# Program order and a new product order at the seams of a Transformer block on one Trainium2 core

## Chip, cores and metric

One core of one Trainium2 chip runs the kernel in one launch. The metric is the device time in microseconds (us); lower is better. TensorE (PE) does the matmuls, VectorE (DVE), ScalarE (ACT) and GpSimd (POOL) prepare operands and finish results, and SyncE (SP) issues most DMAs.

## The reference

One encoder block on x of 1024 tokens x 1024, float32. What matters here is its second half:

```python
merged = sigmoid(ga) * (att @ w_att_up) + sigmoid(gh) * (rec @ w_hgrn_up)
h = layer_norm(ALPHA * h + merged @ w_o, ln1_g, ln1_b)
gate, up = split(h @ w_ffn_in, 2)                      # 1024 x 2816 each
h = layer_norm(ALPHA * h + (silu(gate) * up) @ w_ffn_out, ln2_g, ln2_b)
```

## The kernel before

**Products.** Every float32 operand is split into a high part (a cast to fp32r, on ACT) and a low part (operand less high part, on POOL or DVE: `split`, L201). `mm3` (L227) multiplies high x high, high x low and low x high. The feed-forward projections don't multiply blocks as they are: they use Strassen's scheme in Winograd's form, with seven products in the place of eight, numbered 1 to 7 (`PRODUCTS`, L1258), of sums and differences of blocks. For the input projection the sums of h are b11, b21, t1, t2, b22, t3, t4 (`xb`), those of the weights a11, a12, s1 to s4, a22.

**Output projection** (`phase2`). `wo_chunk` (L1134) loads and splits w_o in chunks of 128 columns. For each tile t of 128 rows two `half`s of 24 matmuls run, then `rest(t, y)` does the first layer norm, transposes the row tile on TensorE in eight 128x128 blocks, evacuates them (`tsv`; `on_act` says which on ACT), and `h1_blocks` makes of them the blocks of the next projection: t1 and t2 at once, b22, t3 and t4 through a store and a load (`td`, `t_raw`). At tile 7 products 1 and 2 of the first two feed-forward groups are started ahead of `rest`.

**Feed-forward input** (`ffn_in`). There are 22 groups, each of two weight columns of 128 (`f_raw`) and seven products of 12 matmuls. `wino_project` (L1319) gives a group in parts; the next group's product 5 stands ahead of the last product, 4, of the one before. `keep` copies a bank to `wkeep`; `evac` makes silu(gate) x up, and `combine` (L1416) the sums a11, a12, a22, s1 to s4 for the last projection, which go to DRAM (`gd`).

**Last projection** (`out_begin`, `ffn_out`). The six products in `OUT_ORDER` have 11 steps each (j = 0 to 10, 66 in all; a step is four `mm3`, 12 matmuls). `sums(s + 2)` and `prep(s + 2)` prepare the weights two steps ahead: a DVE sum, `w_hi` on ACT, `w_lo` on POOL; `acts` loads the activations, for products 5, 7 and 3 split already, as `ghi` and `glo` on the queue of SP. Product 3, the last one, makes beside it the blocks t4 for product 4 (`later`: `t4hi` on ACT, `t4lo` on DVE). Then product 4 runs a row tile at a time for rows 4 to 7. `add` takes the banks to the rows `y2`, `stat` their statistics; `finish` (L1617) is the layer norm of a row tile: a power on POOL, an activation on ACT, a multiply by g2 on POOL (L1629), an add of b2 on DVE (L1630), a store. Row 7 is done on DVE alone. Rows 0 to 6 finish beside product 4.

**What sets the order.** Up to the last projection a scheduler places instructions by its own rules and the given priorities (`high_priority`). From `ffn_out` on `in_order` (L1483) keeps each engine, SP's queue too, to the order in which the code records.

Of the kernel before, what the change touches and what calls it, by code (L numbers as in the profile page):

```python
# [10 lines left out]
F32 = mybir.dt.float32  # L11
# [70 lines left out]
class Block:  # L82
# [1051 lines left out]
    def wo_chunk(self, hl, c):  # L1134
# [5 lines left out]
        self.split(hi[:, :, s], lo[:, :, s], raw)  # L1140

    def phase2(self):
        nc = self.nc
        gc, bc = self.col["g1"], self.col["b1"]
        with ExitStack() as es:
# [54 lines left out]
            raws = []  # L1200

            def rest(t, y):

                with self.tc.high_priority(offset=2 * self.evac_ahead if t == 7 else 0):
                    mv = self.stats(yp, y, "1")
                    if t == 7:
                        nc.vector.tensor_scalar(y, y, mv[:, 0:1], mv[:, 2:3], op0=OP.subtract, op1=OP.mult)
                    else:
                        self.normalise(yp, y, y, mv)
                    on = (0, 1, 3, 4, 6, 7) if 4 <= t < 7 else (1, 3, 4, 6)  # L1210
                    self.h1_blocks(yp, t, lambda q, v=None: self.transposed(yp, y, q, gc, bc, v, on_act=on),
                                   last=t >= 3)
                nc.scalar.dma_start(self.n1_d[t], y)

            for t in range(8):
                ms = []
                for k0 in (0, 4):
# [8 lines left out]
                    ms += [(mh[:, k, :], ml[:, k, :]) for k in range(4)]  # L1226
                y = yp.tile([128, D], F32, name="y1", tag="y1", bufs=2)
                nc.sync.dma_start(y, self.ahs_d[t])

                def half(hh, y=y, ms=ms, t=t):  # L1230
                    ps = self.ps_pj()
                    for k, (mh, ml) in enumerate(ms):
                        whi, wlo = (z[:, k, :] for z in wo[hh])
                        self.mm3(ps, mh, ml, whi, wlo, k == 0, k == KT - 1)
                    s = slice(HALF * hh, HALF * (hh + 1))
                    with self.tc.high_priority(offset=self.evac_ahead if t == 7 else 0):
                        nc.vector.scalar_tensor_tensor(y[:, s], ps, 0.5, y[:, s], op0=OP.mult, op1=OP.add)

                half(0)
                if t == 0:  # L1240
                    second = half, y
                    continue
                if t == 1:
                    second[0](1)
                    rest(0, second[1])
                half(1)
                if t in (5, 6):
                    raws.append(self.ffn_raws(FS[t - 5]))
                if t == 7:
                    self.first_groups = [self.wino_project(raws[f], lambda *a, f=f: self.first_evac[f](*a), 1 + f)  # L1250
                                         for f in range(2)]
                    for g in self.first_groups:
                        next(g)
                rest(t, y)


# [7 lines left out]
    def h1_blocks(self, pool, t, v, last=False):  # L1264
# [9 lines left out]
        if t < 4:  # L1274
            for i, n in enumerate(("b11", "b21")):
                put(n, v(i))
            return
# [14 lines left out]
        less(t1, b12, 0, "b11")  # L1292
        b22 = v(1)
        nc.vector.tensor_sub(t2, b22, t1)
        put("t2", t2)
        put("t1", t1)
        t3 = tmp()
        (nc.vector if last else nc.gpsimd).tensor_sub(t3, b22, b12)
        later(1, "t3", t3)
        later(0, "b22", b22)  # L1300

        t4 = tmp()
        hi, lo = (z[:, :, c].bitcast(F32) for z in self.xb["b21"])
        nc.vector.tensor_sub(t4, hi, t2)
        nc.vector.tensor_add(t4, t4, lo)
        later(2, "t4", t4)
# [12 lines left out]
    def wino_project(self, raws, evac, ahead=0):  # L1319

# [6 lines left out]
        banks = {}  # L1327

        def product(n, bank, first):
            a, b = self.PRODUCTS[n]  # L1330
            hi, lo = self.granules()
            self.split(hi, lo, self.wino_a(A, a))
            xhi, xlo = self.xb[b]
            if first:
                banks[bank] = self.ps_pj() if (bank == 2) != (ahead == 2) else self.ps_sd()
# [6 lines left out]
        def keep(ps):  # L1342
            with self.tc.high_priority(offset=self.evac_ahead):
                t = self.ws.tile([128, HALF], F32, name="wkeep", tag="wkeep", bufs=3)
# [7 lines left out]
        if not ahead:  # L1352
            m5 = keep(product(5, 2, True))
            yield
        m1 = keep(product(1, 1, True))
        c11 = product(2, 3, True)
        if ahead:
            yield
            m5 = keep(product(5, 2, True))
        out(0, 0, c11, m1)  # L1360
        u2 = keep(product(6, 1, False))
        out(0, 1, product(3, 2, False), u2)
# [12 lines left out]
    def ffn_in(self):  # L1375

        nc = self.nc
        with ExitStack() as es:
# [37 lines left out]
            def combine(j, second):  # L1416
# [8 lines left out]
                whole("a12", j, a12)  # L1425
                parts("a22", j, a22)
                s1, s2, s4 = (small(n) for n in ("s1", "s2", "s4"))
                nc.vector.tensor_add(s1, a21, a22)
                nc.vector.tensor_sub(s2, s1, a11)
                nc.vector.tensor_sub(s4, a12, s2)  # L1430
                whole("s2", j, s2)
                parts("s1", j, s1)
                parts("s4", j, s4)

            def vecs(v):
                t = fp.tile([128, D], F32, name=f"ab{len(ab)}")
# [4 lines left out]
            for i, n in enumerate(("b22", "t3", "t4")):  # L1441
                for k in range(4):
                    r = small("t_raw", F32 if k % 2 else F32R).bitcast(F32)
                    nc.sync.dma_start(r, self.td[i][:, k, :])
                    hi, lo = self.xb[n]
                    self.split(hi[:, k, :], lo[:, k, :], r, eng_lo="dve")
            ab = []
            held = None
            for p in range(NF):
                if p > 1:  # L1450
                    grp = self.wino_project(nxt, evac_of(FS[p]))
                    next(grp)
                else:
                    grp = self.first_groups[p]
                if 1 < p + 1 < NF:
                    nxt = self.ffn_raws(FS[p + 1])
                if held:
                    next(held, None)
                    combine((p - 1) // 2, (p - 1) % 2)
# [12 lines left out]
            self.out_begin()  # L1472
            next(held, None)
            combine(NJ - 1, 1)
# [3 lines left out]
    OUT_ORDER = (1, 2, 6, 5, 7, 3)  # L1478
# [4 lines left out]
    def in_order(self):  # L1483
# [4 lines left out]
        for i in traced[n:]:  # L1488
            before = self.lasts.get(i.engine)
# [18 lines left out]
    def out_begin(self):  # L1508

        self.W = W = {}  # L1510
        for i in range(2):
            r = self.wraw.tile([128, D], F32, name="w_raw", tag="wraw", bufs=2)
            for k in range(2):
# [246 lines left out]
```

## Time and profile before

| | us |
|---|---|
| median of 3 runs (lowest to highest) | 2146.92 (2145.78 to 2148.17) |
| the profiled execution | 2148.89 |
| its span | 2147.1 |
| TensorE busy | 2032.1 (95%) |
| VectorE, ScalarE, GpSimd busy | 1394.1, 918.8, 1214.0 |
| mean granted TensorE clock | 0.984 |

Times in the profile are counted from the span's start. A row of an engine has start, duration, engine, line, operation, output and inputs, and in brackets the idle time before it and what ended it. Matmuls are pipelined, so a matmul's duration is longer than the distance to the next.

### The profile page before, as it was taken

The page shows a single profiled execution, that of the slowest core. Times are in us where ns is not written, and L with a number is a line of the kernel's source. Part 1 is how long each engine was busy: PE and PEld are TensorE (multiplying, and loading weights), DVE is VectorE, ACT ScalarE, POOL GpSimd, SP SyncE. Part 2 cuts the span into 40 slices and gives each one's busy share as a digit, 9 for nine tenths or more (in the row PEclk, how much of TensorE's full clock was granted, in tenths as well). Part 3 has the DMA queues.
Part 4 walks back from the last instruction along what each step waited for, and adds up shares of the span by engine and source line. Part 5 has one row for each costly group of instructions (what it writes and reads, how often), then busy time and mean ns, then how long its engine had stood idle before and what let it go on. Part 6 is the DMA issues. An engine that isn't in the chain of part 4 may idle for free.

```text
span 2147.1 us, 31283 instructions
## 1 busy us (share of the span) xinstructions
PE 2032.1 (95%) x10941; PEld 1675.5 (78%) x10941; DVE 1394.1 (65%) x2165; ACT 918.8 (43%) x1870; POOL 1214.0 (57%) x960
## 2 busy tenths in 40 slices
PE   4789999989999999999999899998999999999997
PEld 3678887878778888778888688876788888878876
DVE  7666746876458854778535723347778788867655
ACT  6534455444554435544354432144434344344322
POOL 3465653666535764466644854343567677754554
PEclk9899999999999999999999999999999999999999
DMA  5333442434324453333444764344535444458584
GB/s 205 102 125 103 133 155 93 144 111 158 128 89 143 132 164 121 113 123 117 152 127 137 264 204 157 97 138 141 178 118 177 152 158 158 142 173 292 197 264 156
DMA packets 296447, 324.20 MB, mean 151 GB/s; under 512 B 15905, under 2 KB 212834, under 8 KB 296290
## 3 DMA queue, kind: packets, MB, share of 16 engines
q1 hardware_dynamic: 288832, 296.81, 43.1%
q10 hardware_dynamic: 7458, 25.40, 3.0%
q8 instruction: 86, 1.41, 0.3%
q14 instruction: 71, 0.58, 0.1%
HBM read 211.78 MB, written 110.36 MB: 150 GB/s over the span
## 4 chain that ended last, share of the span: by engine, by line
PE 59%; DVE 5%; issue 4%; DMA 4%; POOL 3%; ACT 2%; SPq 0%; DVEq 0%; ACTq 0%; POOLq 0%
PE pj L229 12%; PE pj L230 12%; PE pj L231 12%; PE sd L231 5%; PE sd L229 5%; PE sd L230 5%; POOL w_lo L208 2%; PE sd L1023 1%; ACT p L801 1%; DVE p L823 1%; DMA wa<-in_w_in_dram 1%; POOL y L1629 1%; DVE hR L984 0%; DMA binb<-in_ln_in_b_dram 0%; PE sd L628 0%
## 5 line engine op out<-in xcount | busy, mean ns | idle before, releaser
L208 POOL TENSOR_TENSOR w_lo<-wa,w_hi 128x512 fp32r<-128x512 f32 x276 | 386.7, 1409 | 278.4 <-ACT w_hi L204 249.2
L204 ACT CAST w_hi<-wa 128x512 fp32r<-128x512 f32 x276 | 170.1, 618 | 230.9 <-PE pj L230 163.6
L208 POOL TENSOR_TENSOR w_lo<-wsum,w_hi 128x512 fp32r<-128x512 f32 x88 | 135.4, 1548 | 79.0 <-ACT w_hi L204 41.4
L208 POOL TENSOR_TENSOR w_lo<-f_raw,w_hi 128x512 fp32r<-128x512 f32 x66 | 109.0, 1664 | 68.0 <-ACT w_hi L204 64.4
L229 PE MATMUL pj<-xt1hi,w_hi 128*128 128x512 f32 x268 | 108.7, 406 | 24.1 <-ACT xt1hi L204 16.7
L230 PE MATMUL pj<-xt1lo,w_hi 128*128 128x512 f32 x268 | 107.8, 402 | 4.5 <-DVE xt1lo L208 4.5
L231 PE MATMUL pj<-xt1hi,w_lo 128*128 128x512 f32 x268 | 107.0, 399 | 0.0
L231 PE MATMUL pj<-xb22hi,w_lo 128*128 128x512 f32 x268 | 104.9, 391 | 2.0 <-POOL w_lo L208 2.0
L463 POOL TENSOR_TENSOR wa<-wa,wa 128x512 f32<-128x512 f32 x46 | 64.5, 1403 | 73.7 <-DVE ws L462 62.2
L229 PE MATMUL pj<-xb22hi,w_hi 128*128 128x512 f32 x268 | 105.7, 394 | 0.1
L230 PE MATMUL pj<-xb22lo,w_hi 128*128 128x512 f32 x268 | 104.8, 391 | 0.0
L208 POOL TENSOR_TENSOR w_lo<-ws,w_hi 128x512 fp32r<-128x512 f32 x46 | 67.3, 1468 | 63.6 <-ACT w_hi L204 63.2
L208 POOL TENSOR_TENSOR w_lo<-Wb,w_hi 128x512 fp32r<-128x512 f32 x47 | 64.7, 1376 | 65.5 <-ACT w_hi L204 64.3
L485 ACT COPY wkeep<-pj 128x512 f32<-128x512 f32 x138 | 80.3, 582 | 11.4 <-DVE evh L377 5.9
L229 PE MATMUL pj<-xb11hi,w_hi 128*128 128x512 f32 x188 | 77.5, 413 | 7.0 <-DVE wkeep L402 5.4
L388 DVE TENSOR_TENSOR evh<-wkeep,pj 128x512 f32<-128x512 f32 x48 | 32.6, 680 | 76.9 <-PE pj L231 56.8
L204 ACT CAST w_hi<-wsum 128x512 fp32r<-128x512 f32 x88 | 54.6, 621 | 65.2 <-PE sd L230 61.9
L229 PEld LDWEIGHTS pj<-xt1hi,w_hi 128*128 128x128 f32 x268 | 52.0, 194 | 37.7 <-ACT xt1hi L204 17.4
L1393 ACT ACTIVATE fth<-fc 128x512 f32<-128x512 f32 x44 | 27.8, 632 | 121.0 <-DVE fc L1392 121.0
L975 ACT ACTIVATE hS<-hR,dec 128x128 f32<-128x128 f32 x112 | 44.5, 402 | 79.8 <-DVE hR L984 57.6
L462 DVE TENSOR_TENSOR ws<-wa,wa 128x512 f32<-128x512 f32 x46 | 39.3, 856 | 60.6 <-DMA wa<-in_w_in_dram 42.3
L229 PE MATMUL pj<-xt4hi,w_hi 128*128 128x512 f32 x188 | 75.3, 401 | 3.0 <-DVE evh L377 3.0
(420 smaller groups left out, 6744.9 us busy)
## 6 DMA issues: line engine op xcount, KB each, us to landing
wa<-in_w_in_dram SPq DMA_DIRECT2D x184, 256.0 KB, 3.0
f_raw<-in_w_ffn_in_dram SPq DMA_DIRECT2D x44, 512.0 KB, 4.1
Wb<-in_w_ffn_out_dram SPq DMA_DIRECT2D x40, 256.0 KB, 4.2
tg<-evh SPq DMA_DIRECT2D x32, 256.0 KB, 3.2
tg<-tg SPq DMA_DIRECT2D x16, 512.0 KB, 3.7
y<-ahs SPq DMA_DIRECT2D x16, 512.0 KB, 4.9
ah<-xt ACTq DMA_DIRECT2D x8, 512.0 KB, 5.8
rec<-hg ACTq DMA_DIRECT2D x8, 512.0 KB, 3.8
```

The source lines that it names most:

```text
L204: nc.scalar.copy(hi, src)
L208: e.tensor_sub(lo, src, hi.bitcast(F32))
L229: nc.tensor.matmul(ps, whi, xhi, start=first, stop=False, **kw)
L230: nc.tensor.matmul(ps, whi, xlo, start=False, stop=False, **kw)
L231: nc.tensor.matmul(ps, wlo, xhi, start=False, stop=last, **kw)
L388: nc.vector.tensor_add(t, add, ps)
L462: nc.vector.tensor_add(a["s1"], a["a21"], a["a22"])
L463: nc.gpsimd.tensor_sub(a["a21"], a["a11"], a["a21"])
L485: nc.scalar.copy(t, ps)
L801: nc.scalar.activation(z, z, AF.Exp, bias=N0[p, hd, tt:tt + 1], scale=QSCALE, accum_out=L0[p, hd, tt:tt + 1])
L975: nc.scalar.activation(S[:, c, :], E, AF.Copy, scale=dec[:, 1, c:c + 1])
L1393: nc.scalar.activation(th[:, s], c[:, s], AF.Tanh, scale=0.5)
```

## The change

The low half of the second half of w_o is split on VectorE. From the last tile's first half to the start of the later feed-forward groups everything is recorded in program order, and the first two groups run side by side (`wino_ahead`), with the splits of b22, t3 and t4 between their parts. `h1_blocks` gives t1 back first and makes the rest later. `combine` is cut into parts, and the first four steps of the last projection are prepared and issued with the last group (`out_begin`). Product 3 comes before product 7; product 7 is the one beside which t4 is made, and beside which rows 0 to 3 are finished whole. At the end rows 4 and 5 go the old way, row 6 and row 7 are done on VectorE. The core of the diff:

```diff
-                self.wo_chunk(wo[1], c)
+                self.wo_chunk(wo[1], c, "dve")
...
+            self.lasts = {}
+            with self.in_order():
+                half(7, 0)
+                rest = turn(6)
+                self.first_groups = [self.wino_ahead(raws[f], lambda *a, f=f: self.first_evac[f](*a), f)
+                                     for f in range(2)]
+                next(self.first_groups[0])
+                half(7, 1)
+                norm(7)
+                rest()
+                next(self.first_groups[0])
+                next(self.first_groups[1])
+                turn(7)()
...
+    def wino_ahead(self, raws, evac, f):
+
+        prep, product, keep, out = self.wino_parts(raws, evac, f == 1)
+        prep(1)
+        prep(2)
+        yield
         m1 = keep(product(1, 1, True))
         c11 = product(2, 3, True)
-        if ahead:
-            yield
-            m5 = keep(product(5, 2, True))
+        prep(5)
+        yield
         out(0, 0, c11, m1)
+        prep(6)
+        m5 = keep(product(5, 2, True))
         u2 = keep(product(6, 1, False))
+        prep(3)
+        prep(7)
+        yield
         out(0, 1, product(3, 2, False), u2)
         out(1, 1, product(7, 1, False), m5)
         yield
...
+            g0, g1 = self.first_groups
+            with self.in_order():
+                splits = late_block(0)
+                next(g1)
+                splits += late_block(1)
+                next(g0)
+                for f in splits[:4]:
+                    f()
+                next(g1)
+                nxt = self.ffn_raws(FS[2])
+                for f in splits[4:]:
+                    f()
+                splits = late_block(2)
+                next(g0)
+                for f in splits:
+                    f()
+                next(g1)
+                next(g0, None)
+            combine(0, 0)
...
-    OUT_ORDER = (1, 2, 6, 5, 7, 3)
+    OUT_ORDER = (1, 2, 6, 5, 3, 7)
...
+            prep(0)
+            next(held, None)
+            prep(1)
+            self.out_step(0, *ready[0])
+            prep(2)
+        with self.in_order((mybir.EngineType.SP,)):
+            combine(NJ - 1, 1, 0)
+        with self.in_order():
+            self.out_step(1, *ready[1])
+            prep(3)
+        with self.in_order((mybir.EngineType.SP,)):
+            combine(NJ - 1, 1, 1)
+            self.out_step(2, *ready[2])
+            combine(NJ - 1, 1, 2)
+            self.out_step(3, *ready[3])
...
+            def whole(t):
+                y = Y[t]
+                self.normalise(rp, y, y, moments(t))
+                nc.gpsimd.tensor_mul(y, y, V[0])
+                ends.append(t)
+                if len(ends) > 1:
+                    end()
...
+            def end():
+                t = ends.pop(0)
+                nc.vector.tensor_add(Y[t], Y[t], V[1])
+                store(t)
...
-                    if p == 3 and j:
+                    if p == 7 and j:
                         later(j - 1)
...
-                    if todo and (p != 2 or j >= NJ - 4):
-                        f, *a = todo.pop(0)
-                        f(*a)
+                    self.out_step(s, *ready.pop(s))
+                    for _ in range(2 if p == 7 else 1):
+                        if todo and (p != 2 or j >= NJ - 4):
+                            f, *a = todo.pop(0)
+                            f(*a)
...
+                    if p == 3:
+                        todo = [a for r in range(4) for a in (todo[r], todo[4 + r])]
+                        todo += [(whole, r) for r in range(4)]
...
-                    if t < 3:
-                        done(4 + t)
-                    else:
-                        ends.pop(0)()
-                        finish(7)
+                finish(7, halves)
```

The order of instructions on GpSimd at the end, before: the eleven splits `w_lo` of product 3, and then the finishes of the rows (`y_17943` is row 0, `y_17970` row 1, `y_18387` row 4).

```order
L208 TENSOR_TENSOR w_lo<-Wb_18212,w_hi 128x512
L208 TENSOR_TENSOR w_lo<-Wb_18239,w_hi 128x512
L208 TENSOR_TENSOR w_lo<-Wb_18267,w_hi 128x512
L1614 TENSOR_TENSOR mv_19203<-mv_19203,mhalf 128x1
L1629 TENSOR_TENSOR y_17943<-y_17943,gb_18695 128x1024
L1614 TENSOR_TENSOR mv_19210<-mv_19210,mhalf 128x1
L1629 TENSOR_TENSOR y_17970<-y_17970,gb_18695 128x1024
L1614 TENSOR_TENSOR mv_19221<-mv_19221,mhalf 128x1
L1629 TENSOR_TENSOR y_18387<-y_18387,gb_18695 128x1024
```

And after, with the splits of product 7's steps j = 6 (`Wb_17857`), 7, 8, 9 and 10:

```order
L208 TENSOR_TENSOR w_lo<-Wb_17857,w_hi 128x512
L1724 TENSOR_TENSOR mv_19015<-mv_19015,mhalf 128x1
L1733 TENSOR_TENSOR y_17940<-y_17940,gb_18694 128x1024
L1724 TENSOR_TENSOR mv_19022<-mv_19022,mhalf 128x1
L1733 TENSOR_TENSOR y_17967<-y_17967,gb_18694 128x1024
L208 TENSOR_TENSOR w_lo<-Wb_17884,w_hi 128x512
L1724 TENSOR_TENSOR mv_19056<-mv_19056,mhalf 128x1
L1733 TENSOR_TENSOR y_17994<-y_17994,gb_18694 128x1024
L1724 TENSOR_TENSOR mv_19065<-mv_19065,mhalf 128x1
L1733 TENSOR_TENSOR y_18021<-y_18021,gb_18694 128x1024
L208 TENSOR_TENSOR w_lo<-Wb_17911,w_hi 128x512
L208 TENSOR_TENSOR w_lo<-Wb_17938,w_hi 128x512
```

The finishes of rows 0 to 3 now stand ahead of the splits of steps 7 and 8, two and two. On SP's queue the stores of these rows stand among the loads of product 7's activations; `gs3h_269` and `gs3l_270` are those of step 6, `_271` and `_272` of step 7, `_273` and `_274` of step 8. Before, all rows were stored after the last such load.

```order
L1668 DMA ghi<-gs3h_269 128x512
L1668 DMA glo<-gs3l_270 128x512
L1728 DMA out_dram<-y_17940 128x1024
L1668 DMA ghi<-gs3h_271 128x512
L1668 DMA glo<-gs3l_272 128x512
L1728 DMA out_dram<-y_17967 128x1024
L1728 DMA out_dram<-y_17994 128x1024
L1668 DMA ghi<-gs3h_273 128x512
L1668 DMA glo<-gs3l_274 128x512
L1668 DMA ghi<-gs3h_275 128x512
```

Each pair of loads now comes behind a store that waits for its row. On ScalarE at the start of the feed-forward, before (from the last cast for products 1 and 2 on; each `w_hi<-wsum` is the high part for one of the products 5, 6, 3 and 7, whose weights are sums):

```order
L204 CAST w_hi<-f_raw 128x512
L204 CAST xt1hi<-tsum 128x4x128
L204 CAST w_hi<-wsum 128x512
L204 CAST xt2hi<-tsum 128x4x128
L1345 COPY wkeep<-sd 128x512
L204 CAST w_hi<-wsum 128x512
L1213 DMA n_114<-y_13720 128x1024
L1393 ACTIVATE fth<-fc 128x512
L204 CAST w_hi<-wsum 128x512
L1345 COPY wkeep<-pj 128x512
L267 ACTIVATE tsv<-sd,vc 128x128 x2
L204 CAST w_hi<-wsum 128x512
```

After, a later piece: from the cast for the first group's product 6 (`w_hi<-wsum`, first row) to that of the second group's.

```order
L204 CAST w_hi<-wsum 128x512
L1378 COPY wkeep<-pj 128x512
L1378 COPY wkeep<-sd 128x512
L204 CAST w_hi<-wsum 128x512 x2
L204 CAST xb22hi<-t_raw 128x512 x4
L1448 ACTIVATE fth<-fc 128x512
L204 CAST w_hi<-wsum 128x512
```

Between these two casts stand the keeps of the first group's products 5 and 6, the casts of its products 3 and 7, and the block b22; before, the first such casts came after one another with keeps, a tanh and the blocks t1 and t2 between, and b22 later.

## Rows read from the trace of the kernel before

**Rows 1.** The page: the span, and the busy time of each engine.

```profile
span 2147.1 us, 31283 instructions
...
PE 2032.1 (95%) x10941; PEld 1675.5 (78%) x10941; DVE 1394.1 (65%) x2165; ACT 918.8 (43%) x1870; POOL 1214.0 (57%) x960
```

**Rows 2.** Waits of PE from 1376 us to the end: total, times, longest.

```profile
PE pj L229 <- ACT xt1hi L204: 8.7, 1, 8.7
PE pj L229 <- ACT w_hi L204: 3.2, 1, 3.2
PE pj L230 <- POOL wo1lo L208: 1.7, 1, 1.7
...
PE pj L229 <- ACT wo1hi L204: 1.5, 1, 1.5
```

**Rows 3.** Windows: us, then busy time (records) by engine, granted clock, DMA share, GB/s.

```profile
1376.00:1400.00 24.00, 20.81 (x91) 16.61 (x90) 6.14 (x9) 5.84 (x9) 12.75 (x8) 1.00 0.37 116
1480.00:1525.00 45.00, 33.93 (x140) 26.17 (x139) 38.31 (x50) 21.34 (x40) 21.62 (x15) 0.89 0.52 160
...
1900.00:1930.00 30.00, 25.84 (x106) 20.73 (x105) 16.60 (x20) 11.59 (x21) 13.22 (x10) 0.94 0.57 186
```

**Rows 4.** Timeline of PE: the first matmuls of two products.

```profile
1483.26 0.39 PE L229 MATMUL sd<-xb21hi,w_hi 128*128 128x512 f32 x1
...
1485.98 0.39 PE L229 MATMUL pj<-xb11hi,w_hi 128*128 128x512 f32 x1
```

**Rows 5.** Timeline of POOL: two splits of w_o chunks.

```profile
1385.80 4.76 POOL L208 TENSOR_TENSOR wo1lo<-w_raw,wo1hi 128x1024 fp32r<-128x1024 f32 x2
```

**Rows 6.** Timeline of DVE at the start of the feed-forward.

```profile
1487.83 1.77 DVE L1207 TENSOR_SCALAR y<-y,mv 128x1024 f32<-128x1024 f32 x1
...
1501.71 0.68 DVE L208 TENSOR_TENSOR xt1lo<-tsum,xt1hi 128x512 fp32r<-128x512 f32 x1
```

**Rows 7.** Timeline of ACT there.

```profile
1477.17 1.16 ACT L267 ACTIVATE tsv<-sd,vc 128x128 f32<-128x128 f32 x3 [1.48 <-DVE xt2lo L208]
...
1480.51 0.62 ACT L204 CAST w_hi<-f_raw 128x512 fp32r<-128x512 f32 x1 [0.62 <-PE pj L230]
...
1484.90 0.58 ACT L1345 COPY wkeep<-sd 128x512 f32<-128x512 f32 x1
```

**Rows 8.** Timeline of POOL there.

```profile
1487.68 1.37 POOL L1316 TENSOR_TENSOR wsum<-f_raw 128x512 f32<-128x512 f32 x1
1489.01 1.74 POOL L208 TENSOR_TENSOR w_lo<-wsum,w_hi 128x512 fp32r<-128x512 f32 x1
1493.15 1.26 POOL L208 TENSOR_TENSOR w_lo<-wsum,w_hi 128x512 fp32r<-128x512 f32 x1 [2.40 <-ACT w_hi L204]
```

**Rows 9.** Timelines of POOL and DVE in product 3.

```profile
2074.87 1.29 POOL L208 TENSOR_TENSOR w_lo<-Wb,w_hi 128x512 fp32r<-128x512 f32 x1 [1.44 <-ACT w_hi L204]
...
2075.41 1.29 DVE L208 TENSOR_TENSOR t4lo<-Wb,t4hi 128x512 fp32r<-128x512 f32 x1 [1.44 <-ACT t4hi L204]
```

**Rows 10.** Timelines of POOL and ACT: the finish of a row.

```profile
2108.62 0.55 POOL L1614 TENSOR_TENSOR mv<-mv,mhalf 128x1 f32<-128x1 f32 x1 [11.92 <-DVE mv L1613]
2110.72 2.40 POOL L1629 TENSOR_TENSOR y<-y,gb 128x1024 f32<-128x1024 f32 x1 [1.55 <-ACT y L252]
2113.08 0.55 POOL L1614 TENSOR_TENSOR mv<-mv,mhalf 128x1 f32<-128x1 f32 x1
...
2109.40 1.25 ACT L252 ACTIVATE y<-y,mv 128x1024 f32<-128x1024 f32 x1 [12.36 <-DVE mv L251]
```

**Rows 11.** Tiles ghi and glo, 2040 to 2105 us.

```profile
DMA to landing us min/median/max: 2.5/3.4/5.8
...
DMA to landing us min/median/max: 3.6/4.8/6.3
```

**Rows 12.** Timeline of DVE at the end.

```profile
2137.13 0.68 DVE L1603 TENSOR_TENSOR y<-y,pj 128x512 f32<-128x512 f32 x1
...
2139.81 1.23 DVE L1630 TENSOR_TENSOR y<-y,gb 128x1024 f32<-128x1024 f32 x1 [1.27 <-POOL y L1629]
```

More of the change, by code (lines that the diff above doesn't have):

```diff
@@ L1197, in phase2, with load, prep @@
             for c in range(4, 8):
-                self.wo_chunk(wo[1], c)
+                self.wo_chunk(wo[1], c, "dve")
             yp = es.enter_context(self.pool("yp"))
[L1200 to L1207, printed above, removed]
-                    else:
[L1209 to L1216, printed above, removed]
+            raws, ms, Y, MV = [], {}, {}, {}
+            def load(t):
+                Y[t] = yp.tile([128, D], F32, name="y1", tag="y1", bufs=3)
+                nc.sync.dma_start(Y[t], self.ahs_d[t])
+            def prep(t):
+                ms[t] = []
                 for k0 in (0, 4):
@@ L1225, in phase2 @@
                         self.split(mh, ml, m1[:, k0:k0 + 4, tk])
[L1226 to L1237, printed above, removed]
@@ L1239, in phase2, with half @@
-                half(0)
+                    ms[t] += [(mh[:, k, :], ml[:, k, :]) for k in range(4)]
+            def half(t, hh):
+                ps, y = self.ps_pj(), Y[t]
+                for k, (mh, ml) in enumerate(ms[t]):
+                    whi, wlo = (z[:, k, :] for z in wo[hh])
+                    self.mm3(ps, mh, ml, whi, wlo, k == 0, k == KT - 1)
+                s = slice(HALF * hh, HALF * (hh + 1))
+                if hh == 0:
+                    MV[t] = self.tiny.tile([128, 2, 6], F32, name="bn1", tag="bnst", bufs=3)
+                nc.vector.scalar_tensor_tensor(y[:, s], ps, 0.5, y[:, s], op0=OP.mult, op1=OP.add)
+                nc.vector.bn_stats(MV[t][:, hh, :], y[:, s])
@@ new lines, in norm @@
+            def norm(t):
+                y, st = Y[t], MV.pop(t)
+                mv = self.tiny.tile([128, 4], F32, name="mv1", tag="bnmv", bufs=3)
+                nc.vector.bn_aggr(mv[:, 0:2], st)
+                nc.vector.tensor_scalar(mv[:, 2:3], mv[:, 1:2], LN_EPS, None, op0=OP.add)
+                nc.gpsimd.tensor_tensor(mv[:, 2:3], mv[:, 2:3], self.mhalf[:, 0:1], OP.pow)
+                if t == 7:
+                    for h in range(2):
+                        s = slice(HALF * h, HALF * (h + 1))
+                        nc.vector.tensor_scalar(y[:, s], y[:, s], mv[:, 0:1], mv[:, 2:3], op0=OP.subtract, op1=OP.mult)
+                else:
+                    self.normalise(yp, y, y, mv)
@@ L1240, in phase2, with turn @@
+            def turn(t):
+                on = (0, 1, 3, 4, 6, 7) if t in (4, 5) else (1, 3, 4, 6) if t < 6 else (4, 5, 6, 7)
+                todo = self.h1_blocks(yp, t, lambda q: self.transposed(yp, Y[t], q, gc, bc, None, on_act=on),
+                                      last=t >= 3)
+                nc.scalar.dma_start(self.n1_d[t], Y[t])
+                return todo
+            for t in range(7):
+                prep(t)
+                load(t)
+                half(t, 0)
                 if t == 0:
-                    second = half, y
@@ L1242, in phase2 @@
                     continue
                 if t == 1:
[L1244 to L1253, printed above, removed]
@@ L1292, in h1_blocks, with rest @@
         less(t1, b12, 0, "b11")
+        put("t1", t1)
         b22 = v(1)
[L1294 to L1306, printed above, removed]
+        def rest():
+            nc.vector.tensor_sub(t2, b22, t1)
+            put("t2", t2)
+            t3 = tmp()
+            nc.vector.tensor_sub(t3, b22, b12)
+            later(1, "t3", t3)
+            later(0, "b22", b22)
+            t4 = tmp()
+            hi, lo = (z[:, :, c].bitcast(F32) for z in self.xb["b21"])
+            nc.vector.tensor_sub(t4, hi, t2)
+            nc.vector.tensor_add(t4, t4, lo)
+            later(2, "t4", t4)
+        return rest
     def wino_a(self, A, name):
@@ L1693, in ffn_out @@
                     f(*a)
+                end()
+                for t in range(4, 8):
+                    stat(t, 1)
                 for t in range(4):
```

233 lines of the change are left out of this document (132 added, 101 removed).

## The prediction, made before the changed kernel ran

> **What bounds the kernel.** I read the page first. TensorE is busy 95% of a span of 2147.1 us [rows 1], so what can be won or lost is the time in which TensorE stands still or runs slowly, and a transfer or another engine counts only where TensorE, or the end, waits for it. The profiled execution took 2148.89 us, 1.97 more than the median of the three runs; the sum below is made against this one execution, and I give the predicted time as the median plus the sum.
>
> The waits of TensorE from 1376 us on come next [rows 2]: few and large. The windows give their price with the clock in it [rows 3]. One 128x512 matmul follows the other at 0.2267 us (twelve of them between two products take 2.72) [rows 4]. At that pitch the 91 matmuls of 1376 to 1400 are 20.6 us, so 3.4 were lost at the start of the output projection. In 1480 to 1525, 140 records with 8 short transposes among them (about 0.8 us) are 30.7 us: 14.3 lost, of which 11.1 are idle (45.0 less 33.93 busy) and 3.2 a granted clock of 0.89. In 1900 to 1930, 106 matmuls are 24.0: 6.0 lost. What follows the last matmul is the finish of the last row on VectorE. The rest of TensorE's time is full, and the change adds or removes no matmul.
>
> **A, the low half of the second half of w_o on VectorE.** TensorE waited 1.7 us for wo1lo and 1.5 for wo1hi [rows 2], behind four GpSimd splits of 2.4 us each [rows 5]. A VectorE split of half that width takes about 0.68 [rows 6], so 1.3 for the whole, and VectorE was busy 6.1 us of these 24 [rows 3]. I take **-3** (between 0 and -3.4, all that was lost).
>
> **B, the two groups side by side.** I follow the new order from T0 = 0, the end of the last tile's second half. Casts on ScalarE take 0.62, four evacuations 1.55, a keep 0.58 [rows 7]; a VectorE tensor operation about 0.68, its follower 0.6 later, the normalising 1.77 [rows 6]; a GpSimd split 1.26, or 1.74 beside VectorE, and the third sum 1.37 [rows 8].
> - VectorE, from the half that ended at -6.4, has two splits, the statistics, four evacuations of tile 6 and four sums ahead of t1: ready at -0.2. ScalarE casts it by +0.5, evacuates four blocks by 2.0, and only then casts the first weights, 2.6; their low part is done at 3.95. TensorE's first product needs it with its third matmul: 3.5 lost. Products 1 and 2 and the transposes end at 10.0.
> - The next weights stand on ScalarE behind xt2hi of tile 6 and the cast of a sum that VectorE makes after the normalising (7.7) and six more operations: 11.8. So 13.0 for the cast, 15.2 for the low part behind another: 4.7 lost. The other group's products 1 and 2 and product 5 end at 22.9.
> - Product 6 needs s2, which VectorE reaches after all of tile 7's blocks: 23.6, cast 24.3, low part 25.6: 2.3 lost. Product 6 ends at 27.9, the other product 5 at 30.6.
> - The other product 6 has on ScalarE ahead of it the keep of the first product 6 (28.5), a cast (29.1), a cast that waits for two GpSimd operations (31.8), and four casts of block b22 (34.6); then an add, the tanh, two VectorE operations (37.9), cast and low part, 39.9: 8.9 lost, since only one product of 2.72 lies beside that chain.
> - The first product 7 needs block t3, whose casts stand behind a cast that waits for a GpSimd sum: 48.0 against 44.9: 3.3 lost.
>
> That is 22.7. The slow clock cost 3.2 in the old seam after its wait of 8.7 [rows 2, 3]; I add 3.5 for a wait as long and four shorter ones. 26 against 14.3: **+12**. If each of the dozen GpSimd operations in it took 0.45 more, as beside VectorE, it would be +18. If all waits but the first were covered it would be -10. The later groups keep their order in substance: 0, as TensorE is full there.
>
> **C, four steps of the last projection prepared ahead.** Now step 0 is cast before the last product 4 and runs behind it, steps 1 to 3 follow between the parts of the combine. The 3.2 and the pitch loss vanish: **-5.8** (-4 if one low part is late).
>
> **D, product 7 last, with rows 0 to 3 finished beside it.** Time 0 is product 7's first step, each step is 12 matmuls, 2.72. In a step VectorE makes the weight block (0.65), ScalarE casts it and the t4 block (2 casts), GpSimd splits the one, VectorE the other. The row that bears on this: a t4lo that began at 2075.41, in the middle of a GpSimd split (2074.87, 1.29), ended 0.54 after it [rows 9]. With it the add and the statistic of one row, 1.3, come behind, so a step is 0.65 + 0.1 + 0.62 + 0.1 + 1.29 + 0.54 + 1.3, about 4.5 where TensorE takes 2.72. After four adds and statistics and the t4lo of the fifth step, GpSimd's first power stands at P = 17.5 (11.5 if no t4lo met a split).
>
> One row's finish on GpSimd runs at 4.46: power 0.55, VectorE, ScalarE 1.25, multiply 2.40, the next power [rows 10]. In program order GpSimd now has two rows, the split of step 7 (counted from 0), two rows, the split of step 8. Step 7's split ends at P + 2 x 4.46 + 1.3 = P + 10.2. On the queue of SP the store of row 0 stands ahead of the activations of step 7, and it waits for VectorE's add at P + 6.5; a landing takes 3.4 and 4.8 [rows 11], so P + 11.7. Step 7 is wanted at 19.0. For step 8: two more rows and two splits, P + 21.5, and the stores of rows 1 and 2 ahead of its activations, P + 23.0, which its third matmul needs: it starts at about P + 22.5 = 40.0, where 21.8 is wanted. Two further steps have all they need soon after. **+18** (at least 10: P = 11.5, GpSimd's passes and splits alone, 31.9 against 22.2; at most 22: P at 18.5 and landings at their longest). In the kernel before nothing waited here, because those rows came under product 4, when no split was left.
>
> The Trainium skill (SBUF — State Buffer, "SBUF: two separate sides") says that a VectorE operation with two SBUF inputs and a GpSimd operation that reads SBUF exclude each other for a whole instruction. The t4lo row agrees. By that rule a multiply of 2.40 also holds up the weight block of steps 7 and 8 when it starts first.
>
> **E, the end.** Before, the last row's add began at 2137.13, without idle time behind the b2 add of row 5; with the statistic it was done two operations of 0.68 later, 2138.5. But VectorE then took row 6's b2 add at 2139.81, for which it waited for GpSimd's multiply, 1.23 long, ahead of row 7's finish [rows 12]. Row 6 is now done on VectorE alone, in the 7.5 us (33 matmuls) that product 4 takes per tile. So row 7's finish begins 2.5 earlier (2138.5 against 2141.0), and its add up to 1.2 earlier, of which I take 0.7: **-3.2** (0 to -3.7).
>
> **Sum.** -3 + 12 - 5.8 + 18 - 3.2 = +18: 2146.9 + 18 = **2165 us** (2167 against the profiled execution).
>
> **Rivals.**
> 1. *The other side: the pairing covers its waits.* Place: TensorE's products 6 in the first two groups. If the second group's s2 is cast before TensorE ends its product 5, each group's wait lies under the other's products and B is -10, not +12: 2143, no difference that can be told. If the finish of four rows also costs only its lower bound of 10, 2135. For it: 11 us of the old seam are plain idle, which another product can fill. Against: the b22 casts stand ahead of that cast on ScalarE, and 2.72 us are all that lies beside. It decides where s2 of the second group is ready less than 33 us after T0.
> 2. *GpSimd's multiplies hold VectorE's blocks.* Each of two blocks waits up to 2.4, and so do two adds: D is 22 to 28, 2169 to 2175, with B at +18 up to 2181. For it: the t4lo row. Against: step 8 waits for its activations anyway.
> 3. *The finish beside product 7 hides.* That would take P + 22.5 below 22: the passes alone rule it out, unless the finishes slip behind product 7; in the new program order they don't.
>
> **Chances.** Forecast 0.60 (2154 to 2176); rival 2 0.13; pairing covered, D as worked out 0.15 (0.03 of it faster, 0.10 same, 0.02 slower); covered and D short 0.10; other slower 0.02. A change of under 0.2% (4.3 us) is about what a measurement of this kernel can't tell from none. So faster 0.13, same 0.10, slower 0.77. The range 2144 to 2180 leaves out rival 1's faster part and the top of rival 2.
>
> **What would show it.** Right: TensorE waits of 7 to 10 and about 8 us in the steps 7 and 8 of product 7, released by GpSimd's split or by ghi and glo, with two multiplies ahead of each; a wait of 7 us or more before the second product 6; none above 1 us between product 4 and the last projection; no VectorE wait for GpSimd before row 7's finish. Wrong: those steps full, or the first groups' losses under 14 us together.

## The result, and the profile after

| us | before | after |
|---|---|---|
| median (lowest to highest), 4 runs each | 2147.55 (2145.78 to 2151.34) | 2176.18 (2174.96 to 2180.56) |
| the profiled execution | 2148.89 | 2176.61 |
| its span | 2147.1 | 2174.8 |
| mean granted TensorE clock | 0.984 | 0.980 |

After over before is 1.0135 (95% interval 1.0115 to 1.0154): slower by 28.6 us. Forecast were 2165 (+18) and a range of 2144 to 2180. The page of after, against [rows 1]:

```profile
span 2174.8 us, 31264 instructions
...
PE 2046.9 (94%) x10941; PEld 1682.7 (77%) x10941; DVE 1392.7 (64%) x2172; ACT 916.1 (42%) x1867; POOL 1200.0 (55%) x955
```

As many matmuls as before, and 14.8 us more of busy TensorE: part of the loss is a slower clock, since a matmul at the low clock counts as busy. The waits of TensorE in after from 1376 us on (total, times, longest), against [rows 2]:

```profile
PE pj L229 <- DMA ghi<-gs3h: 12.7, 3, 7.0
PE pj L229 <- ACT w_hi L204: 9.1, 2, 8.5
PE sd L229 <- ACT w_hi L204: 8.9, 3, 4.3
PE sd L229 <- ACT xt3hi L204: 2.1, 1, 2.1
PE pj L231 <- POOL w_lo L208: 1.8, 1, 1.8
...
PE pj L229 <- ACT wo1hi L204: 0.7, 1, 0.7
PE pj L230 <- DVE wo1lo L208: 0.5, 1, 0.5
```

The 8.7 for xt1hi and the 3.2 before the last projection are gone. In their place stand waits for operands at six places in the first two groups and two large ones for `ghi` in product 7. The windows say what each place costs; their columns are those of [rows 3]. First after:

```profile
1376.00:1400.00 24.00, 22.81 (x99) 18.24 (x98) 11.53 (x14) 7.22 (x13) 4.93 (x7) 1.00 0.39 121
...
1475.00:1550.00 75.00, 51.21 (x173) 37.57 (x172) 39.53 (x61) 26.22 (x50) 22.54 (x18) 0.82 0.35 112
...
1914.00:1944.00 30.00, 29.22 (x129) 23.87 (x128) 18.15 (x22) 12.67 (x22) 14.98 (x11) 1.00 0.45 151
2100.00:2136.00 36.00, 23.26 (x81) 17.55 (x80) 20.60 (x33) 12.22 (x17) 19.20 (x13) 0.81 0.38 130
```

And product 3 of before, which stood where product 7 stands now:

```profile
2075.00:2105.00 30.00, 29.66 (x129) 23.46 (x129) 24.10 (x28) 9.87 (x18) 11.89 (x8) 1.00 0.73 226
```

By the prediction's reckoning (records at 0.2267, short transposes at 0.1):

| term | lost before | lost after | change | forecast |
|---|---|---|---|---|
| A, output projection | 3.4 | 24 - 99 x 0.2267 = 1.6 | -1.8 | -3 |
| B, first groups | 14.3 | 75 - (165 x 0.2267 + 0.8) = 36.8 | +22.5 | +12 |
| C, start of the last projection (at 1923.8 before, 1937.3 after) | 6.0 | 30 - 129 x 0.2267 = 0.8 | -5.2 | -5.8 |
| D, the product beside t4 | 30 - 129 x 0.2267 = 0.8 | 36 - 81 x 0.2267 = 17.6 | +16.8 | +18 |
| E, last matmul to the end | 10.9 | 7.7 | -3.2 | -3.2 |

Together +29.1, against a difference of the spans of 27.7. The two executions differ by 2.4 us even ahead of the change: the first matmul with w_o starts at 1383.4 in before and at 1381.0 in after. Counted from there the difference is 30.1, so no sum here is truer than some 2 us.

**D.** After's GpSimd and the queue of SP around steps 7 and 8 of product 7 (L1724 is the power, L1733 the multiply, L1728 a store):

```profile
2104.19 0.55 POOL L1724 TENSOR_TENSOR mv<-mv,mhalf 128x1 f32<-128x1 f32 x1 [0.93 <-DVE mv L1723]
2106.29 2.37 POOL L1733 TENSOR_TENSOR y<-y,gb 128x1024 f32<-128x1024 f32 x1 [1.55 <-ACT y L252]
...
2113.27 1.71 POOL L208 TENSOR_TENSOR w_lo<-Wb,w_hi 128x512 fp32r<-128x512 f32 x1
...
2121.45 2.58 POOL L1733 TENSOR_TENSOR y<-y,gb 128x1024 f32<-128x1024 f32 x1 [1.55 <-ACT y L252]
2123.99 1.71 POOL L208 TENSOR_TENSOR w_lo<-Wb,w_hi 128x512 fp32r<-128x512 f32 x1
```
```profile
2110.53 0.34 SPq L1728 DMA_DIRECT2D out_dram<-y  x1
2110.96 0.38 SPq L1668 DMA_DIRECT2D ghi<-gs3h  x1
...
2116.84 4.75 SPq L1728 DMA_DIRECT2D out_dram<-y  x2
2121.69 0.38 SPq L1668 DMA_DIRECT2D ghi<-gs3h  x1
```

TensorE there: the first matmul of step 7, a later one, and the first of step 8.

```profile
2114.54 0.77 PE L229 MATMUL pj<-w_hi,ghi 128*128 128x512 f32 x1 [7.04 <-DMA ghi<-gs3h]
...
2117.33 0.63 PE L229 MATMUL pj<-w_hi,ghi 128*128 128x512 f32 x1
2117.76 0.63 PE L230 MATMUL pj<-w_lo,ghi 128*128 128x512 f32 x1
...
2125.38 0.77 PE L229 MATMUL pj<-w_hi,ghi 128*128 128x512 f32 x1 [5.46 <-DMA ghi<-gs3h]
```

Each `ghi` is issued right behind the store of a row, 2110.96 and 2121.69, lands 3.6 and 3.7 later, and the matmul starts. GpSimd's split for step 8 ends at 2125.70, 21.5 behind the first power: the forecast's P + 21.5. Of the 17.6 lost here 12.7 are idle; the rest is slow clock, for which the forecast had no term in D. After each wait the matmuls stand 0.43 apart instead of 0.227, the lower of the clock's two levels, 1.2 GHz for 2.4.

**B.** The last matmul of the output projection makes way for the next at T0 = 1476.2. From there TensorE's idle times are, in order of time, 4.0 (3.5 forecast), 2.5 (4.7), 4.3 before the first product 6 (2.3), 8.5 before the second (8.9), 3.0 before the first product 7 (3.3), and 1.2 that the forecast hasn't: 23.5 against 22.7. So the waits were nearly those foretold in sum, but the window loses 13.0 more than its idle time of 75 - 51.21 = 23.8. That is slow clock, for which the forecast had 3.5: behind the first five waits the matmuls ran slowly for a while, which cost 2.0, 1.7, 3.2, 3.0 and 2.0, together some 12 of the 13 (time from the wait's end to the full pitch, less further idle time, less the records at 0.2267). The expectations below count the waits from the start of one matmul to that of the next, less the pitch: 4.3, 2.7, 4.4, 8.6, 3.5 and 1.4. TensorE behind the 4.3 (a matmul in the later ones lasts 0.63 for 0.39):

```profile
1505.69 0.80 PE L229 MATMUL sd<-xt2hi,w_hi 128*128 128x512 f32 x1 [4.27 <-ACT w_hi L204]
...
1508.92 0.63 PE L229 MATMUL sd<-xt2hi,w_hi 128*128 128x512 f32 x1
1509.34 0.63 PE L230 MATMUL sd<-xt2lo,w_hi 128*128 128x512 f32 x1
```

Why that wait was 4.3 and not 2.3 shows on VectorE, in the chain that leads to s2 of the first group:

```profile
1498.59 0.68 DVE L1346 TENSOR_TENSOR wsum<-f_raw 128x512 f32<-128x512 f32 x1
1502.25 0.69 DVE L1447 TENSOR_TENSOR fc<-wkeep,sd 128x512 f32<-128x512 f32 x1 [2.98 <-DMA td<-tsum]
```

The add neither reads nor writes `tsum`, yet the store of a `tsum` block ended its wait. By the code `fc` is made when the room of `tsum` has been given back; I take it that the add writes memory that this block held, and waits until the store has read it. The forecast followed the operands alone.

### The profile page after: what moved, and what is told of

Same layout as the page of the kernel before. It is cut to its first block, busy times and chain, and to the rows that moved or that the text cites. A ratio compares the mean times of both kernels' runs of the same rounds, so it can differ in the third digit from the quotient of the medians.

```text
span 2174.8 us, 31264 instructions
## 1 busy us (share of the span) xinstructions
PE 2046.9 (94%) x10941; PEld 1682.7 (77%) x10941; DVE 1392.7 (64%) x2172; ACT 916.1 (42%) x1867; POOL 1200.0 (55%) x955
## 5 line engine op out<-in xcount | busy, mean ns | idle before, releaser
L229 PE MATMUL pj<-xt2hi,w_hi 128*128 128x512 f32 x188 | 76.2, 406 | 8.5 <-ACT w_hi L204 8.5
L231 PE MATMUL pj<-xt2hi,w_lo 128*128 128x512 f32 x188 | 75.6, 402 | 3.7 <-POOL w_lo L208 3.5
```

Of the source, the lines that this page charges most:

```text
L229: nc.tensor.matmul(ps, whi, xhi, start=first, stop=False, **kw)
L231: nc.tensor.matmul(ps, wlo, xhi, start=False, stop=last, **kw)
```

## The experiments

Beside the medians I use one length from the profiles: from T0 to the first matmul of product 4 in the last projection. It is 624.4 in before and 659.6 in after, and leaves out what varies ahead of T0. It varies itself: experiment 8, whose code behind T0 is that of before, has 626.6, and of the kernels that share after's first groups, after and experiments 5, 6 and 7, the time from T0 to the last projection is 461.4, 462.4, 459.6 and 459.5. So some 3 us between two profiles tell nothing.

**1. The old code from the last row tile on (e8_oldseam).** B undone; A, C, D and E kept. `phase2`, `h1_blocks`, `wino_project` and the first groups in `ffn_in` are those of before:

```diff
-            self.lasts = {}
-            with self.in_order():
-                half(7, 0)
-                rest = turn(6)
...
-                turn(7)()
+                if t == 7:
+                    self.first_groups = [self.wino_project(raws[f], lambda *a, f=f: self.first_evac[f](*a), 1 + f)
+                                         for f in range(2)]
+                    for g in self.first_groups:
+                        next(g)
+                rest(t, y)
```

> The changed kernel with the old code from the last row tile to the start of the later feed-forward groups (priorities and scheduler in place of program order, products 5 and 6 group after group); w_o's low half stays on VectorE, the last projection stays new. Theory (the new seam loses 37 us where the old lost 15): 2176 less 22, 2154 (2152 to 2156). Rival (what is lost at the seam is won back from the later groups, which start better prepared): 2160 to 2166.

Measured: 2153.43 us (2150.67 to 2156.06), 1.0026 of before [1.0015, 1.0036]. From T0 to product 4 it is 636.6, 23.0 less than after. The price of B stands by undoing it.

**2. Dummy matmuls in the wait before the second product 6 (e6_fill).** 38 matmuls into a bank whose content nobody reads; the outputs are not touched.

```diff
+        if f == 1:
+            fill, z = self.ps_pj((self.npj + 1) % 4), self.xb["b11"][0]
+            for i in range(38):
+                self.nc.tensor.matmul(fill, z[:, i % 4, 0:128], z[:, i % 4, :], start=i == 0, stop=i == 37)
         u2 = keep(product(6, 1, False))
```

> The changed kernel with 38 matmuls more, whose results nobody reads, on TensorE in the wait of 8.6 us before the second group's product 6. Theory (after that wait TensorE runs at 1.2 GHz for some 5.4 us, which costs 3): product 6 begins within 0.5 us of where it did, its matmuls follow at 0.2267 us at once, 2173 to 2174. Rival (the wide pitch after the wait comes from operands that arrive late): no change, 2176, with 0.43 us pitch in spite of the extra matmuls.

Measured: 2171.12 us (2169.94 to 2174.07), 1.0116 [1.0088, 1.0143], but only 1.1 less from T0 to product 4 (658.5), which is no gain that can be told; the rest lies ahead of T0. TensorE in the filler (L1416), behind it, and at a later wait:

```profile
1509.45 8.77 PE L1416 MATMUL pj<-xb11hi 128*128 128x512 f32 x38
...
1520.95 0.39 PE L230 MATMUL pj<-xt2lo,w_hi 128*128 128x512 f32 x1
1521.18 0.39 PE L231 MATMUL pj<-xt2hi,w_lo 128*128 128x512 f32 x1
...
1539.54 0.50 PE L229 MATMUL sd<-xt4hi,w_hi 128*128 128x512 f32 x1 [1.91 <-ACT w_hi L204]
...
1542.08 0.63 PE L229 MATMUL sd<-xt4hi,w_hi 128*128 128x512 f32 x1
1542.51 0.63 PE L230 MATMUL sd<-xt4lo,w_hi 128*128 128x512 f32 x1
```

The matmuls behind the filler stood 0.227 apart, so the slow stretch there does follow from the idle time. But the products then reached the next operands earlier, waited 1.9 before a product 4 where after waited 1.2, and ran slowly behind that, where after hadn't. And not every wait leaves a slow stretch: the second one, 3.0 in all here as in experiment 4, left none, where 2.5 at that place left one in after.

**3. Dummy matmuls in three waits (e13_fill3).** As 2, and 15 and 22 more ahead of the first product and the first product 6 (the diff is against experiment 2).

```diff
+        if f == 0:
+            fill, z = self.ps_pj((self.npj + 1) % 4), self.xb["b11"][0]
+            for i in range(15):
+                self.nc.tensor.matmul(fill, z[:, i % 4, 0:128], z[:, i % 4, :], start=i == 0, stop=i == 14)
...
-        if f == 1:
+        if True:
...
-            for i in range(38):
+            for i in range((22, 38)[f]):
```

> The changed kernel with matmuls whose results nobody reads in three of the waits of the new seam: 15 before the first product 1, 22 before the first product 6, 38 before the second. Theory (of the 37 us that the seam loses, 12 are TensorE at 1.2 GHz behind waits, which I had put at 3.5): the products begin where they did, and the wide pitch behind these three waits goes: 5 to 7 us less at the seam than in the changed kernel, 2169 to 2172. Rival (TensorE then only waits longer for the next operand, since VectorE, ScalarE and GpSimd go at their own speed): the wide pitch goes but the seam's length stays within 2 us, 2174 to 2176.

Measured: 2172.64 us (2168.82 to 2174.63), 1.0105 [1.0080, 1.0131], between the range expected and the rival's; 654.9 from T0 to product 4, 4.7 less than after, of which the spread above can be 3. The three filled places ran at the full pitch; the second wait, not filled, grew from 2.5 to 3.6, the one before product 7 stayed (3.1 for 3.0), and slow stretches followed both. The three stretches had cost 2.0, 3.2 and 3.0, so of 8.2 at most 4.7 came back.

**4. The second group's preparation earlier (e5_seam).** The sums for product 6 stand ahead of the other group's products 5 and 6, block b22 behind.

```diff
         prep(6)
+        yield
         m5 = keep(product(5, 2, True))
         u2 = keep(product(6, 1, False))
+        yield
...
                 next(g0)
+                next(g1)
+                next(g0)
                 for f in splits[:4]:
                     f()
+                next(g0)
                 next(g1)
```

> The changed kernel with the first two feed-forward groups paired further: the second group's first sum and the cast for its product 6 come ahead of the first group's products 5 and 6, and b22 is split behind them. Theory (the 8.6 us before the second product 6 are ScalarE's program order: a keep, two casts and b22 ahead of the cast that TensorE waits for): that wait goes with its slow clock and the waits at products 7 shrink, 2176 less 12 to 18, 2158 to 2164; the first three waits (4.3, 2.7, 4.4) stay. Rival (the sums on VectorE and GpSimd are the bound, whatever ScalarE's order): the wait moves to products 3 and 7, 2170 or more.

Measured: 2169.11 us (2166.56 to 2170.52), 1.0100 [1.0084, 1.0116]: a miss. From T0 to product 4 it is 651.8, 7.8 less than after. The 8.5 is gone, but the first product 6 waits 5.5 for 4.3, and TensorE's waits in 1470 to 1550 now read:

```profile
PE sd L229 <- ACT w_hi L204: 14.9, 4, 5.8
PE pj L231 <- POOL w_lo L208: 2.5, 3, 1.8
```

and one of them, 5.8 before a product 4, stands behind ScalarE's casts of the t4 block, which waited 3.6 for their load:

```profile
1533.27 2.69 ACT L204 CAST xt4hi<-t_raw 128x512 fp32r<-128x512 f32 x4 [3.63 <-DMA t_raw<-td]
```

In this order, by the program, the step that went ahead put others back. Whether another order of the two groups covers more wasn't tried.

**5. Rows 0 to 3 out of product 7 (e1_tail).** D's finish undone: row 0 stands at the end of product 7, the others beside product 4.

```diff
+                    if p == 7 and j == NJ - 2:
+                        whole(0)
...
-                        todo += [(whole, r) for r in range(4)]
...
-                    if t in (1, 2):
-                        whole(3 + t)
-                        end()
+                    for r in ((1,), (2, 3), (), ())[t]:
+                        whole(r)
                     if t == 3:
+                        end()
```

> The changed kernel with the finishes of rows 0 to 3 taken out of the middle of product 7: row 0 is finished in step 9, when no split is left for GpSimd, the others beside product 4. Theory (the finishes hold up the splits and the loads of steps 7 and 8, 17 us): about 2160 us (2158 to 2163), with no wait above 1 us in product 7; one or two of the 17 stay, because a step still needs 3.2 us from the weight block to t4lo where TensorE takes 2.72. Rival (a step of product 7 is bound by its own chain of VectorE, ScalarE and GpSimd, about 4.5 us): 2170 or more, with the waits spread over steps 6 to 10.

Measured: 2168.56 us (2166.43 to 2169.55), 1.0100 [1.0077, 1.0122]: 7.6 less than after, where more was expected. The two waits for `ghi` are gone; a new one stands at product 4. A wait of TensorE in 2060 to 2145, and two of VectorE's sums of weights in product 7:

```profile
PE pj L229 <- DVE y L1713: 4.9, 1, 4.9
```
```profile
2094.01 0.68 DVE L1691 TENSOR_TENSOR Wb<-Wb,Wb 128x512 f32<-128x512 f32 x1
...
2098.58 0.67 DVE L1691 TENSOR_TENSOR Wb<-Wb,Wb 128x512 f32<-128x512 f32 x1
```

VectorE's step takes 4.57 where TensorE's takes 2.72. While one row's add and statistic share each of the first four steps (behind them a step takes 3.24), the t4 blocks and the last adds fall behind, and product 4 waits for them. That is a second cost of the new product order, which the forecast had counted only as the way to P: once the finish is out, it comes to light.

**6. Sums a step earlier, one addition per step (e11_tail2).** Experiment 5 and:

```diff
-                    sums(s + 2)
+                    for i in (s + 2, s + 3):
+                        if i < len(steps) and (i == s + 3) == (steps[i][0] == 7):
+                            sums(i)
...
-                    for _ in range(2 if p == 7 else 1):
+                    for _ in range(1):
```

> As the run with the finishes out of product 7 (2168.6), and besides the weight sums of product 7 one step earlier on VectorE and one add or statistic per step in the place of two. Theory (what that run kept, a wait of 5.1 us for VectorE's adds at the start of product 4 and a slow clock behind it, comes from the chain sum, cast, t4hi, t4lo of 3.2 to 4.6 us a step that the swap of products 3 and 7 made; with the sum ahead a step needs about 2.6 of VectorE): 2168.6 less 6, 2161 to 2164, with no wait above 1 us in product 7 or at product 4. Rival (VectorE's t4lo behind GpSimd's split is enough to make a step longer than 2.72): 2166 or more, the wait stays.

Measured: 2161.26 us (2156.07 to 2164.24), 1.0070 [1.0051, 1.0088]. No wait above 1 us is left in products 7 and 4:

```profile
2060.00:2145.00 85.00, 84.64 (x370) 68.54 (x368) 53.23 (x75) 23.23 (x34) 42.89 (x30) 1.00 0.71 226
```

85 - 370 x 0.2267 = 1.1 lost. So D is two things, by the medians about 8 for the finish (5) and 7 for VectorE's pace in the new order (6). The earlier sums and the single addition came together; which of them wins how much wasn't tried.

**7. The stores behind the last loads (e2_store).** Rows 0 to 3 are finished as in after, but stored behind the activations.

```diff
-                store(t)
+                if t < 4:
+                    held_back.append(t)
+                else:
+                    store(t)
```

> The changed kernel with only the stores of rows 0 to 3 moved behind the last loads of product 7 on the queue of SP. Theory (GpSimd's splits of steps 7 and 8 end at the same time as the late loads land, so either lock alone keeps TensorE waiting): 2174.5 to 2176.5, with the same two waits, now ended by GpSimd's or ScalarE's weights. Rival (the queue of SP is the cause; the profile of the changed kernel puts 12.7 us of TensorE's waits down to ghi): 2164.

Measured: 2174.17 us (2171.81 to 2175.28), 1.0126 [1.0103, 1.0148]. TensorE's waits in 2060 to 2145:

```profile
PE pj L229 <- ACT w_hi L204: 6.6, 2, 4.1
PE pj L230 <- POOL w_lo L208: 4.7, 2, 2.4
```

The large waits for `ghi` are gone and waits for the weights are in their place: two locks stood one behind the other, as forecast. To open this one wins 2.0 us by the medians and 0.3 from T0 to product 4 (659.3), so nothing that can be told. The other one alone, the finishes off GpSimd with the stores left where they are, wasn't tried.

**8. The low half of w_o alone (e10_wo).** Before, with A only.

```diff
-                self.wo_chunk(wo[1], c)
+                self.wo_chunk(wo[1], c, "dve")
```

> The kernel before with w_o's low half split on VectorE, and nothing else. Theory (TensorE loses 3.8 us there before and 1.8 after): 2 us less than the kernel before, 2145 to 2147, which is near what can be told. Rival (the scheduler moves other work and a later wait takes the place): no difference.

Measured: 2146.03 us (2142.43 to 2149.58, 12 runs) beside 2147.99 for before (17 runs): 0.9989 [0.9980, 0.9999], the 2.0 that was expected, with an interval that all but reaches no difference.

**9. What pays, together (e12_best).** A, C and E of the change, the start of the feed-forward of experiment 1 and the end of experiment 6.

```diff
-            self.lasts = {}
-            with self.in_order():
-                half(7, 0)
...
-                        todo += [(whole, r) for r in range(4)]
+                    if p == 7 and j == NJ - 2:
+                        whole(0)
```

> The last kernel's end (finishes out of product 7, sums a step ahead) with the old seam at the start of the feed-forward: what is left of the change is w_o on VectorE, the four steps ahead, product 3 before 7 and row 6 on VectorE. Theory (A -2, C -6.3, E -3.1, D and B gone): 11 less than the kernel before, 2136 to 2140. Rival (parts of C and E are paid back elsewhere): 2143 or more.

Measured: 2137.03 us (2133.43 to 2140.23, 6 runs) beside 2147.99: 0.9952 [0.9939, 0.9966]. It beats both kernels, before by half a per cent. Of its waits of TensorE the first is before's:

```profile
PE pj L229 <- ACT xt1hi L204: 8.7, 1, 8.7
PE pj L229 <- ACT wkeep L1345: 3.0, 1, 3.0
PE pj L231 <- DMA glo<-gs3l: 1.3, 1, 1.3
```

Read part by part it should gain less: A -2, C -5, E -3, and some 4 still lost in product 7 and ahead of product 4, 6 in all against 11 measured (7 to 13). From T0 to product 4 it is no shorter than before, 624.2 against 624.4: the 4 about offsets what C wins there. T0 falls between 1471.6 and 1479.1 in the profiles of after and of these kernels, so single profiles can't say where the other 5 come from; that stays open.

**10. Dummy matmuls in that 8.7 (e14_best_fill).** Experiment 9, with 38 of them ahead of the first product 5.

```diff
+            if ahead == 1:
+                fill, z = self.ps_pj((self.npj + 1) % 4), self.xb["b11"][0]
+                for i in range(38):
```

> The kernel with the new end and the old seam (2137.0) with 38 matmuls more, whose results nobody reads, in the old seam's wait of 8.7 us. Theory: the 0.43 us pitch behind that wait goes, 2 to 3 us less, 2134 to 2135. Rival (the time is given back at the next wait): 2137.

Measured: 2140.98 us (2136.85 to 2144.97), 0.9963 [0.9946, 0.9979]: no gain over 9, and 624.1 from T0 to product 4 against its 624.2. The products behind the filler ran at the full clock, but a later wait took 5.7, where the next large one of 9 took 3.0 (for `wkeep`):

```profile
PE sd L229 <- ACT w_hi L204: 5.7, 1, 5.7
```

## Why the prediction was right in sign and short in size

- **A, forecast -3, measured -1.8** in the windows and -2.0 by experiment 8. The lock was GpSimd's; a wait of 0.7 for `wo1hi` and one of 0.5 for the low part stay.
- **B, forecast +12, measured +22.5** and 23 by experiment 1. This is the step that failed, and in it one term: "I add 3.5 for a wait as long and four shorter ones". The slow clock took 13.0. The rows of before showed 3.2 behind one wait of 8.7 and two short ones (1.6 and 0.7; the 3.2 of [rows 2] stands at the last projection); the forecast gave five waits the price of one. In after each of the five waits of 2.5 to 8.5 us left a stretch at the low level of its own, and experiments 2 and 3 show that it hangs on the idle time. How it feeds the chain shows on ScalarE, where the keep of the first product 6 stands ahead of the second group's cast:

```profile
1511.72 0.59 ACT L1378 COPY wkeep<-sd 128x512 f32<-128x512 f32 x1 [5.59 <-PE sd L231]
```

That is 35.6 behind T0, where 28.5 was forecast: some 4 because s2 was late, some 3 because product 6 ran slowly. The second product 6 then started at 47.0, where 39.5 follows from the forecast (30.6 and 8.9). The waits themselves were right in sum (22.7 forecast, 23.5 measured), in part by luck: the second was 2.2 shorter than foretold, the third 2.0 longer, since the forecast missed the 2.98 for a store. What B would be without that store wasn't tried.
- **C, forecast -5.8, measured -5.2.** The last projection starts without a wait; what is left is a wait of 0.8 for VectorE, before the product 4 just ahead of it.
- **D, forecast +18, measured +16.8.** Product 7's first matmul starts at 2087.29, so P is 16.9 (17.5 forecast), and step 8 starts at 2125.38, 38.1 behind it (40.0 forecast); VectorE had begun 1.8 ahead of the product, where the first bank of product 3 came free:

```profile
2085.45 0.69 DVE L1713 TENSOR_TENSOR y<-y,sd 128x512 f32<-128x512 f32 x1 [15.58 <-PE sd L231]
...
2087.29 0.39 PE L229 MATMUL pj<-w_hi,ghi 128*128 128x512 f32 x1
```

The waits were 7.0 and 5.5, where 7 to 10 and about 8 were foretold, and the slow clock behind the second cost 2.2 that wasn't: two misses that offset one another, so how near the sum came is in part luck. The mechanism holds: experiment 5 took both locks away and both waits went, experiment 7 took the store's away and the weights still held TensorE. But the reading that only the finish costs was short: without it half of the loss stays, since VectorE's 4.57 us a step, which the forecast had at about 4.5, is too slow for that product anyway.
- **E, forecast -3.2, measured -3.2.** After, the last add begins at the last matmul's end and nothing stands between it and the finish:

```profile
2167.11 0.69 DVE L1713 TENSOR_TENSOR y<-y,pj 128x512 f32<-128x512 f32 x1 [3.64 <-PE pj L231]
2167.84 0.69 DVE L1718 BATCH_NORM_STATS2 bns<-y 128x6 f32<-128x512 f32 x1
```

- **Rival 1 (the pairing covers its waits) fell**: s2 of the second group was cast at 1522.4, 46 behind T0, where less than 33 was its condition. Experiment 4 took that wait away and paid elsewhere.

```profile
1522.44 0.62 ACT L204 CAST w_hi<-wsum 128x512 fp32r<-128x512 f32 x1 [1.42 <-DVE wsum L1346]
```

- **Rival 2 (the multiplies hold VectorE) fell as well**, though the measured 2176 lies in the range that it was given (2169 to 2175, up to 2181 with B at +18): what the forecast lacked came from B's slow clock. GpSimd gave way. The multiply at 2121.45 met a weight sum that had begun first, and took 2.58 where one alone took 2.37. The rule of the Trainium skill (SBUF — State Buffer, "SBUF: two separate sides") that the prediction quoted agrees where VectorE comes second:

```profile
2121.15 0.68 DVE L1691 TENSOR_TENSOR Wb<-Wb,Wb 128x512 f32<-128x512 f32 x1
...
2124.50 1.75 DVE L1691 TENSOR_TENSOR Wb<-Wb,Wb 128x512 f32<-128x512 f32 x1
```

The second sum, 0.68 elsewhere, began within GpSimd's split of 2123.99 and ended at 2126.25, 0.55 behind that split's end.
- **Rival 3 (the finish hides) fell**: the two waits for `ghi` are its price.

## What to carry to other kernels

Price each new wait of TensorE with a slow stretch of its own behind it, not the whole place with one: here 1.7 to 3.2 us for each of five waits, though at one place a wait of 3.0 left none. When work of another kind goes in among the steps of a full product, follow every queue it stands in, the store's too: here two locks held one step, and to open the store's alone gave nothing that could be told. Before moving work under a product, compare that product's step on the helping engine (4.57) with its step on TensorE (2.72): where the helper is slower already, there is no cover.

## What was not expected of the hardware

Keeping TensorE busy through a wait does keep its clock: behind the fillers matmuls stood 0.227 apart, where they stood 0.43 apart without. But the time came back only in part (at most 4.7 of 8.2 us in experiment 3) or not at all (experiments 2 and 10): the faster stretch came to a later operand earlier, idled longer there (1.9 for 1.2 in experiment 2) and slowed down behind that. My reading, not tested further, is that in these runs, where a chain on other engines set the pace, most of the slow stretch only stood in for idle time.
